# A second SwiGLU that starts with Strassen products, and casts in another order

## The chip, the cores and the metric

The kernel runs on one core of one Trainium2 chip. The metric is the device time of one execution in microseconds (us). The engines are TensorE (PE, matmuls), VectorE (DVE), ScalarE (ACT), GpSimd (POOL) and SyncE (SP, which issues most DMAs).

## The reference, cut to what matters

Two layers over 512 tokens with 1024 features, all in float32. Each layer is

```python
h = h + 0.5 * swiglu(rmsnorm(h, ffn1_norm[i]), ffn1_w_gu[i], ffn1_w_down[i])      # ffn1, hidden width 2816
u = rmsnorm(h, mix_norm[i])
...                                      # u @ w_in: conv branch, q/kv latents, two gates
merged = sigmoid(g_conv) * y_conv + sigmoid(g_mla) * y_mla    # y_mla: attention, 8 heads, block causal
h = h + merged @ w_o[i]
h = h + 0.5 * swiglu(rmsnorm(h, ffn2_norm[i]), ffn2_w_gu[i], ffn2_w_down[i])      # ffn2, the same shapes
h = h + sigmoid(rmsnorm(h, ple_norm[i]) @ w_ple_gate[i]) * (p[i] @ w_ple_proj[i])
```

where `swiglu(x) = (silu(x @ w_gate) * (x @ w_up)) @ w_down`. A final RMSNorm follows.

## The kernel before, in words

**Layout.** Everything is transposed: `h` is eight tiles `h[0..7]`, 128 features by 512 tokens each. To keep float32 accuracy on PE every operand is split into a high part (a cast to fp32r, on ACT) and a low part (the difference, on DVE), and one product is three matmuls: high x high, high x low, low x high (`mm3`, lines 212 to 214). Activations go through `split`/`split_to`, weights through `Stream.split` (lines 70 and 71), which handles 1024 columns (eight weight tiles of 128 x 128, a "half") at a time.

**Weights.** `Stream` reads halves from HBM in the order in which the program asks for them, into 10 raw buffers (`st`, and `s` for sums of weights); the cast parts `wh` and `wl` have 4 buffers each (`N_WH`). `W.get` hands out one 128 x 128 tile after another of the current half, so a projection can begin in the middle of a half.

**ffn.** For each hidden tile f of 22 the gate and up columns are multiplied with the normed h. The factor of the norm, `r`, comes from a sum of squares over all features (`Squares`, `rms`, matmuls with ones at lines 291 and 292) and is applied to the results, so the matmuls can begin before it is known. Two f make a pair n. A pair can be done whole (`projs`: 4 column tiles x 8 feature tiles x 3 matmuls of 512 tokens) or with seven Strassen-Winograd products (`Sevens`): tokens are cut in two halves of 256, features in two halves of 4 tiles, columns in two. A product is 4 feature tiles x 2 x 3 = 24 matmuls of 256 tokens. The token operands are built by `Halved.row(j)` out of h[j] and h[j+4]: products 1, 2, 3 take pieces of the normed h, 5 and 7 take halves of `t`, 6 and 4 halves of `u`. Product 1 uses the left half of h[j], product 5 the left half of `t`, which is the right half of h[j] minus its left; the other five need h[j+4]. The weight operands are built by `Quad.part` out of four quarters a11 to a22 on DVE: products 5, 6, 3 and 7 need a sum of weights first, and all seven a split. `step(n, j)` does product j of pair n and drains its PSUM bank; `finish` multiplies with r, applies silu and splits the result.

Before the change ffn2 does the first pair (f = 0, 1) whole (`n_whole = 2`) and pairs 1 to 10 as Strassen products. `early_rows` is off for ffn2: all four rows of `Halved` are built after the whole pair's first projections were issued. From pair 2 on, pieces of the down projection (`down`) stand between the products.

**Mixer.** Gates are Strassen products over four pairs; `conv_out(m)` (12 matmuls of 512 columns, then one DVE product) is placed between them, four for each of the last two pairs. `qkv(pr)` projects two heads: `q_rope` (and its rotation on ACT and DVE, `rope`), `key`, `query`, `values`, and casts each result; `scores` makes four score tiles of 128 queries for one head, 20 matmuls in all, and the softmax; `turn` transposes them, `mix_v` multiplies with the values. At the end W_o is applied for m = 0 to 7 and added into `h[m]`, and the next ffn's `normed` splits and squares each `h[m]` as it comes.

**Order.** PSUM has 8 banks, all from one pool, and the activations 60 tiles from one pool (`G`). A scheduler orders each engine's queue at build time: among the instructions whose operands and buffers are ready by its own estimates it takes the one that comes first in the program. On the chip every queue then runs in that order, and an instruction that waits holds all behind it.

Of the kernel before, what the change touches and what calls it, by code (L numbers as in the profile page):

```python
# [172 lines left out]
def trunk_kernel(ctx, tc, dims, x, p, positions, gains, rope_c, weights, out):  # L173
# [28 lines left out]
    def split_to(hi, lo, src, scale=None):  # L202
        if scale is None:
            nc.scalar.copy(hi, src)
            nc.vector.tensor_tensor(lo, src, hi.bitcast(F32), ALU.subtract)
        else:
            nc.scalar.activation(hi, src, AF.Copy, scale=scale)
            nc.vector.scalar_tensor_tensor(lo, src, scale, hi.bitcast(F32), ALU.mult, ALU.subtract)
# [35 lines left out]
    nc.gpsimd.dma_start(out=cols, in_=gains)  # L244
# [128 lines left out]
    class Halved:  # L373


        def __init__(self, nm, l, name):
            self.nm, self.l, self.name = nm, l, name
            self.ys = {p_: [] for p_ in range(1, 8)}

        def row(self, j, xs):  # L380
            H = S // 2
            left, right = slice(0, H), slice(H, S)
            name, k = self.name, j + KD // 2

            def halves_of(hi_lo, *ps_):
                for at, p_ in zip((left, right), ps_):
                    if p_:
                        self.ys[p_].append(tuple(t[:, at] for t in hi_lo))
# [6 lines left out]
            nc.vector.tensor_tensor(t13[:, left], xj[:, right], xj[:, left], ALU.subtract)  # L395
            nc.vector.tensor_tensor(t13[:, right], xk[:, right], xj[:, right], ALU.subtract)
            nc.vector.tensor_tensor(t24[:, left], t13[:, right], xj[:, left], ALU.add)
            nc.vector.tensor_tensor(t24[:, right], xk[:, left], t24[:, left], ALU.subtract)
            halves_of(split(t13, f"{name}t{j}"), 5, 7)
            halves_of(split(t24, f"{name}u{j}"), 6, 4)  # L400

    class Sevens:
# [17 lines left out]

        def product(self, ps, d, j):
            hi, lo = d["w"].part(j)
# [31 lines left out]
    def ffn(l, nm, name, first=False, beside=None, early=False):  # L454
# [20 lines left out]
        for f in range(n, n_whole):  # L475
            pss += projs(cs[f], xs, names[f])
        for j in range(n_early, KD // 2):
            ys.row(j, xs)

        def activate(f):  # L480
            g, u = G(f"{name}gn{f}"), G(f"{name}un{f}")
            nc.vector.tensor_tensor(g, pss[2 * f], r, ALU.mult)
            nc.scalar.activation(g, g, AF.Silu)
            nc.vector.tensor_tensor(u, pss[2 * f + 1], r, ALU.mult)
            nc.vector.tensor_tensor(u, u, g, ALU.mult)
            acts[f] = split(u, f"{name}a{f}")
# [18 lines left out]

# [504 lines left out]
```

## Time and profile before

| | |
|---|---|
| median of 3 runs | 2289.8 us (2289.72 to 2291.17) |
| the profiled execution | 2290.97 us, of which the span from first to last instruction is 2289.1 us |
| busy: PE, DVE, ACT, POOL | 2276.7, 1796.1, 1161.2, 34.7 us |
| matmuls | 14168 |
| read from HBM | 218.4 MB |

Times in rows are us from the start of the span. A row of the timeline gives start, duration, engine, source line, operation, output and inputs, shape, and in brackets how long the engine had been idle before it and what ended that. Matmuls overlap: the distance between two starts is what one costs, not its duration. The names b0, b1 are ffn2 of layer 0 and 1, a0, a1 ffn1, m0, m1 the mixer; `b01b` is bank b of pair 1 in b0, `m0s10p` the scores of head 0 of head pair 1 in m0.

### The profile page before, as it was taken

How to read it: one execution, taken by the hardware profiler on the slowest of the kernel's cores; microseconds unless marked ns; L12 is line 12 of the kernel's file. 1: busy time of each engine (PE TensorE's matmuls, PEld its weight loads, DVE VectorE, ACT ScalarE, POOL GpSimd, SP SyncE). 2: the span in 40 equal slices, each digit the busy share in tenths (PEclk: the TensorE clock that was granted, in tenths of full speed). 3: DMA queues.
4: the chain of work that ended last, by engine and by line, in shares of the span. 5: the costliest groups of instructions: out<-in, count | busy, mean ns of one | idle time of the engine just before them, and what ended most of it. 6: DMA issues, size and time to landing. Idle time of an engine off the chain costs nothing.

```text
span 2289.1 us, 34697 instructions
## 1 busy us (share of the span) xinstructions
PE 2276.7 (99%) x14168; PEld 2060.7 (90%) x14168; DVE 1796.1 (78%) x2508; ACT 1161.2 (51%) x1744; POOL 34.7 (2%) x43
## 2 busy tenths in 40 slices
PE   9999999999999999999999999999999999999998
PEld 8999988899888999998899999888988889999988
DVE  8887778877876988877798887768878669877765
ACT  7444445455743644444664444445467356444455
POOL 0000000000200000000000000000001000000000
PEclk9999999999999999999999999999999999999999
DMA  5333343134122233233223333322331123333321
GB/s 194 111 111 93 105 130 102 56 110 138 38 65 85 73 111 111 93 119 122 91 83 94 110 98 115 120 90 67 119 104 56 65 74 102 104 100 99 113 83 38
DMA packets 62975, 222.76 MB, mean 97 GB/s; under 512 B 7120, under 2 KB 7120, under 8 KB 62816
## 3 DMA queue, kind: packets, MB, share of 16 engines
q1 hardware_dynamic: 62208, 219.70, 30.4%
q8 instruction: 111, 1.82, 0.3%
q10 hardware_dynamic: 576, 0.79, 0.1%
q14 instruction: 48, 0.39, 0.1%
q0 software_dynamic: 32, 0.05, 0.0%
HBM read 218.42 MB, written 2.10 MB: 96 GB/s over the span
## 4 chain that ended last, share of the span: by engine, by line
PE 97%; DVE 2%; ACT 0%; issue 0%; DMA 0%; ACTq 0%; POOLq 0%
PE a0pd L212 2%; PE b0pd L212 2%; PE a1pd L212 2%; PE b1pd L212 2%; PE b1pd L213 2%; PE a1pd L213 2%; PE b0pd L213 2%; PE a0pd L213 2%; PE b1pd L214 2%; PE a1pd L214 2%; PE a0pd L214 2%; PE b0pd L214 2%; PE e1gp L212 1%; PE e1gp L214 1%; PE e1gp L213 1%; PE m0mop L212 1%
## 5 line engine op out<-in xcount | busy, mean ns | idle before, releaser
L70 ACT CAST wh<-st 128x1024 fp32r<-128x1024 f32 (+1 forms) x455 | 474.7, 1044 | 574.8 <-issue 57.7
L71 DVE TENSOR_TENSOR wl<-st,wh 128x1024 fp32r<-128x1024 f32 (+1 forms) x456 | 552.4, 1212 | 160.3 <-ACT wh L70 159.5
L70 ACT CAST wh<-s 128x1024 fp32r<-128x1024 f32 x94 | 98.8, 1051 | 132.6 <-PE b1pd L213 8.5
L71 DVE TENSOR_TENSOR wl<-s,wh 128x1024 fp32r<-128x1024 f32 x94 | 114.5, 1218 | 15.6 <-ACT wh L70 15.6
L149 DVE TENSOR_TENSOR st<-st,s 128x1024 f32<-128x1024 f32 x47 | 57.5, 1223 | 1.1
L146 DVE TENSOR_TENSOR s<-s,st 128x1024 f32<-128x1024 f32 x47 | 57.3, 1220 | 0.2
L141 DVE TENSOR_TENSOR s<-st,st 128x1024 f32<-128x1024 f32 x47 | 57.3, 1218 | 0.1
L152 DVE TENSOR_TENSOR st<-st,st 128x1024 f32<-128x1024 f32 x47 | 57.2, 1218 | 0.0
L511 DVE SCALAR_TENSOR_TENSOR h<-b0pd,h 128x512 f32<-128x512 f32 x40 | 27.5, 689 | 9.4 <-PE b0pd L214 9.2
L511 DVE SCALAR_TENSOR_TENSOR h<-b1pd,h 128x512 f32<-128x512 f32 x40 | 27.5, 688 | 9.4 <-PE b1pd L214 9.2
L511 DVE SCALAR_TENSOR_TENSOR h<-a1pd,h 128x512 f32<-128x512 f32 x40 | 27.5, 688 | 7.7 <-PE a1pd L214 7.7
L511 DVE SCALAR_TENSOR_TENSOR h<-a0pd,h 128x512 f32<-128x512 f32 x40 | 27.5, 687 | 6.4 <-PE a0pd L214 6.4
L106 POOL MEMSET wh<- 128x256 f32 x4 | 1.1, 313 | 1191.5 <-DVE wl L71 1191.5
L799 DVE TENSOR_TENSOR m1g<-m1mop,m1g 128x512 f32<-128x512 f32 x8 | 5.5, 690 | 6.5 <-PE m1mop L214 6.5
L799 DVE TENSOR_TENSOR m0g<-m0mop,m0g 128x512 f32<-128x512 f32 x8 | 5.5, 690 | 6.5 <-PE m0mop L214 6.5
L295 ACT ACT_TABLE_LOAD x8 | 10.3, 1283 | 0.1
L910 ACT ACTIVATE fsq<-h 128x256 f32<-128x256 f32 (+1 forms) x10 | 4.8, 480 | 9.9 <-DVE h L891 9.9
L804 DVE TENSOR_TENSOR h<-m0wop,h 128x512 f32<-128x512 f32 x8 | 5.5, 691 | 4.1 <-PE m0wop L214 4.1
L804 DVE TENSOR_TENSOR h<-m1wop,h 128x512 f32<-128x512 f32 x8 | 5.5, 690 | 4.1 <-PE m1wop L214 4.1
L621 DVE TENSOR_TENSOR m0z<-m0Vp,m0c 128x512 f32<-128x512 f32 x4 | 2.8, 692 | 6.2 <-PE m0Vp L214 6.2
L621 DVE TENSOR_TENSOR m1z<-m1Vp,m1c 128x512 f32<-128x512 f32 x4 | 2.8, 691 | 6.2 <-PE m1Vp L214 6.2
L650 DVE TENSOR_TENSOR m0g<-m0cop,m0g 128x512 f32<-128x512 f32 x8 | 5.5, 688 | 2.5 <-PE m0cop L214 2.5
(11171 smaller groups left out, 8787.5 us busy)
## 6 DMA issues: line engine op xcount, KB each, us to landing
st<-in_weights SPq DMA_DIRECT2D x406, 512.0 KB, 3.5
h<-in_x SPq DMA_DIRECT2D x8, 256.0 KB, 5.4
st<-in_weights SPq DMA_DIRECT2D x7, 256.0 KB, 5.3
out<-fo SPq DMA_DIRECT2D x7, 256.0 KB, 2.5
e0pi<-in_p SPq DMA_DIRECT2D x2, 256.0 KB, 3.7
e1pi<-in_p SPq DMA_DIRECT2D x2, 256.0 KB, 4.0
st<-in_weights ACTq DMA_DIRECT2D x1, 256.0 KB, 3.7
pos_i<-in_positions ACTq DMA_DIRECT2D x1, 256.0 KB, 3.8
```

What stands on the lines that cost most here:

```text
L70: self.nc.scalar.copy(hi[:, w], src[:, w])
L71: self.nc.vector.tensor_tensor(lo[:, w], src[:, w], hi[:, w].bitcast(F32), ALU.subtract)
L141: tt(self.s, self.a21, self.a22, ALU.add)
L146: tt(self.s, self.s, self.a11, ALU.subtract)
L149: tt(self.a12, self.a12, self.s, ALU.subtract)
L152: tt(self.a11, self.a11, self.a21, ALU.subtract)
L212: nc.tensor.matmul(ps, wh, vh, start=first, stop=False)
L213: nc.tensor.matmul(ps, wh, vl, start=False, stop=False)
L214: nc.tensor.matmul(ps, wl, vh, start=False, stop=last)
L511: nc.vector.scalar_tensor_tensor(h[m], ps, 0.5, h[m], ALU.mult, ALU.add)
L799: nc.vector.tensor_tensor(t, mla_ps[m], t, ALU.mult)
L804: nc.vector.tensor_tensor(h[m], ps, h[m], ALU.add)
```

## The change

1. **ffn2 in Strassen products from the first pair on** (`early=3`, `n_whole = 0`). `Halved.row` is cut in two: `own(j)` needs h[j] alone, `other(j)` needs h[j+4] too. During W_o `early_rows` calls `own` for rows 0 to 3 as h[0..3] come, and `other` for rows 0 to 2 as h[4..6] come; after h[6] the weight operands of products 1 and 5 of pairs 0 and 1 are split ahead (`sevens.split`). After h[7] comes `other(3)`. PE then does (0,1), (0,5), the sum of squares, (1,1), (1,5), and only then (0,2), (0,6), (0,3), (0,7), (0,4), (1,2), (1,6), (1,3) and the rest as before.
2. **Order by hand.** `tc.issue_after(ins)` puts what its block traces on the engine of `ins` behind `ins` in that engine's queue. The ACT drains of the first four products stand behind the multiplication for row 3; the DVE work of the other products up to (1,3), with the weight sums and splits, stands behind the last split of row 3 (`sums`).
3. **Mixer.** `conv_out(7)` moves from between the gate products to behind `qkv(0)`, ahead of the first scores. Since it hands out four weight tiles, `qkv(0)` now begins in the middle of a half, and its `values` come after the second query. In every `qkv` the two rotated query parts and the splits of the values are traced after all other parts.
4. **Launch.** The table of gains `cols` is loaded by SP, as its first DMA, where POOL did it.
5. ffn1 and the mixer build their rows through `own` and `other`, one behind the other: the same operations, `y` multiplied after the first difference.

The core of the diff:

```diff
-    nc.gpsimd.dma_start(out=cols, in_=gains)
+    nc.sync.dma_start(out=cols, in_=gains)
...
         def row(self, j, xs):
+            self.own(j, xs)
+            self.other(j, xs)
+        def own(self, j, xs, parts=False):
...
-            xj, xk, t13, t24 = (G(f"{name}{w}{j}") for w in "xytu")
-            nc.scalar.mul(xj, h[j], gain(self.nm, self.l, j))
-            nc.scalar.mul(xk, h[k], gain(self.nm, self.l, k))
-            halves_of(xs[j], 1, None)
-            halves_of(xs[k], 2, 3)
...
+            x, t = G(f"{self.name}x{j}"), G(f"{self.name}t{j}")
+            nc.scalar.mul(x, h[j], gain(self.nm, self.l, j))
+            nc.vector.tensor_tensor(t[:, left], x[:, right], x[:, left], ALU.subtract)
+            th, tl = G(f"{self.name}t{j}h", F32R), G(f"{self.name}t{j}l", F32R)
+            if parts:
+                split_to(th[:, left], tl[:, left], t[:, left])
+            self.ys[1].append(tuple(v[:, left] for v in xs[j]))
+            self.ys[5].append((th[:, left], tl[:, left]))
+            self.half[j] = x, t, th, tl, parts
+        def other(self, j, xs):
+            H = S // 2
+            left, right = slice(0, H), slice(H, S)
+            k = j + KD // 2
+            x, t, th, tl, parts = self.half.pop(j)
+            y, u = G(f"{self.name}y{j}"), G(f"{self.name}u{j}")
+            x_ins = nc.scalar.mul(y, h[k], gain(self.nm, self.l, k))
+            nc.vector.tensor_tensor(t[:, right], y[:, right], x[:, right], ALU.subtract)
+            nc.vector.tensor_tensor(u[:, left], t[:, right], x[:, left], ALU.add)
+            nc.vector.tensor_tensor(u[:, right], y[:, left], u[:, left], ALU.subtract)
+            at = right if parts else slice(0, S)
+            split_to(th[:, at], tl[:, at], t[:, at])
+            uh, ul = G(f"{self.name}u{j}h", F32R), G(f"{self.name}u{j}l", F32R)
+            last = split_to(uh, ul, u)
+            for p_, v, at in ((2, xs[k], left), (3, xs[k], right), (7, (th, tl), right), (6, (uh, ul), left), (4, (uh, ul), right)):
+                self.ys[p_].append(tuple(w[:, at] for w in v))
+            return x_ins.ins, last.ins
...
+        def split(self, n, j):
+            if n not in self.todo:
+                self.todo[n] = self.quad(n)
+            self.todo[n]["part", j] = self.todo[n]["w"].part(j)
         def product(self, ps, d, j):
-            hi, lo = d["w"].part(j)
+            hi, lo = d.pop(("part", j), None) or d["w"].part(j)
...
-    def ffn(l, nm, name, first=False, beside=None, early=False):
+    def ffn(l, nm, name, first=False, beside=None, early=2):
...
-        n_early = KD // 2 - 2 if early else 0
-        def early_rows(k, xs):
-            if KD // 2 < k + 1 <= KD // 2 + n_early:
-                ys.row(k - KD // 2, xs)
...
-        xs, acc = normed(nm, l, name, early_rows)
...
-        n_whole = 4 if first else 2
-        cs = [[W.col(nm + "_w_gu", l, c + f * P, D) for c in (0, DFF)] for f in range(n_whole)]
-        names = [[f"{name}p{w}{f}" for w in "gu"] for f in range(n_whole)]
-        n = 2 if first else 1
-        pss = projs(sum(cs[:n], []), xs, sum(names[:n], []), first)
-        r = rms(acc, D, name)
...
+        n_whole = 4 if first else 0 if early > 2 else 2
+        n0 = n_whole // 2
...
+        def early_rows(k, xs):
+            j = k - KD // 2
+            if n_whole == 0:
+                if j < 0:
+                    ys.own(k, xs, True)
+                elif j < early:
+                    ys.other(j, xs)
+                if k == KD - 2:
+                    for n in range(2):
+                        for j in (1, 5):
+                            sevens.split(n, j)
+            elif 0 <= j < early:
+                ys.row(j, xs)
+        xs, acc = normed(nm, l, name, early_rows)
+        if n_whole == 0:
+            x_ins, sums = ys.other(KD // 2 - 1, xs)
+            with tc.issue_after(x_ins):
+                step(0, 1)
+                step(0, 5)
+            r = rms(acc, D, name)
+            with tc.issue_after(x_ins):
+                step(1, 1)
+                step(1, 5)
+            order = (2, 6, 3)
...
+            for f in range(n, n_whole):
+                pss += projs(cs[f], xs, names[f])
+            for j in range(early, KD // 2):
+                ys.row(j, xs)
+            order = (1, 2, 5, 6, 3)
...
         np_ = nf // 2
-        n0 = n_whole // 2
         for f in range(n_whole - 2):
             activate(f)
-        step(n0, 1)
-        activate(n_whole - 2)
-        step(n0, 2)
-        step(n0, 5)
-        activate(n_whole - 1)
-        step(n0, 6)
-        step(n0, 3)
+        with tc.issue_after(sums) if n_whole == 0 else nullcontext():
+            for j in order:
+                if n_whole and j in (2, 6):
+                    activate(n_whole - (2 if j == 2 else 1))
+                step(n0, j)
...
             between = [(lambda m=m, f0=f0: down(m, f0, f0 + 4)) for m in range(4 * (n % 2), 4 * (n % 2) + 4)] if n > 1 else []
             for i, (n_, j_) in enumerate(((n + 1, 1), (n, 7), (n + 1, 5), (n, 4), (n + 1, 2), (n + 1, 6), (n + 1, 3))):
-                step(n_, j_)
+                if n == n_whole == 0:
+                    if j_ not in (1, 5):
+                        with tc.issue_after(sums):
+                            step(n_, j_)
+                else:
+                    step(n_, j_)
                 if i in (1, 2, 3, 5) and between:
                     between.pop(0)()
...
-            between = [(lambda m=m: conv_out(m)) for m in range(4 * n - 4, 4 * n)] if n else []
+            between = [(lambda m=m: conv_out(m)) for m in range(4 * n - 4, min(4 * n, KD - 1))] if n else []
             order = [(n + 1, 1), (n, 7), (n + 1, 5), (n, 4)]
             order += [(n + 1, j) for j in ((6, 2, 7, 3, 4) if n + 1 == n_last else (2, 6, 3))]
...
-                    vs.append(split(ps, f"{n}v{tb}"))
+                    vs.append(ps)
                 res["v"] = vs
...
-            def q_rope_parts():
+            def q_rope_parts(t):
                 qr = res["qr"]
...
-            query0 = lambda: query(0)
-            parts = [(3, q_rope), (2, lambda: key(0)), (3, query0), (2, lambda: key(1)), (3, lambda: query(1))]
+            parts = [(3, q_rope), (2, lambda: key(0)), (3, lambda: query(0)), (2, lambda: key(1)), (3, lambda: query(1))]
             at = [i for i in range(1, len(parts) + 1) if W.pairs_fit(2, sum(w for w, _ in parts[:i]))]
             parts.insert(at[-1], (4, values))
             for _, part in parts:
                 part()
-                if part is query0:
-                    q_rope_parts()
+            for t in range(2):
+                q_rope_parts(t)
+            res["v"] = [split(ps, f"{n}v{2 * i}") for i, ps in enumerate(res["v"])]
             return res
...
         qk = qkv(0)
+        conv_out(KD - 1)
         es = [scores(0, t, qk) for t in range(2)]
...
-        ffn(l, "ffn1", f"a{l}", l == 0, rotary if l == 0 else None, l > 0)
+        ffn(l, "ffn1", f"a{l}", l == 0, rotary if l == 0 else None, 2 if l else 0)
         mixer(l)
-        ffn(l, "ffn2", f"b{l}")
```

## Rows read from the trace of the kernel before

**Rows 1.** The page: busy time of the engines, and the granted clock of PE in 40 slices of the span (tenths of full speed, 9 is 90% or more).

```profile
PE 2276.7 (99%) x14168; PEld 2060.7 (90%) x14168; DVE 1796.1 (78%) x2508; ACT 1161.2 (51%) x1744; POOL 34.7 (2%) x43
...
PEclk9999999999999999999999999999999999999999
```

**Rows 2.** The waits of PE over the whole span: who waited for whom, us in total, times, longest.

```profile
PE a0pg L230 <- ACT a0x0h L207: 1.6, 1, 1.6
...
PE m0s10p L734 <- DVE m0h1qn1l L205: 0.9, 1, 0.9
PE m1s10p L734 <- DVE m1h1qn1l L205: 0.9, 1, 0.9
```

**Rows 3.** Timeline of PE from the end of W_o in layer 0: the first whole matmul of ffn2, the sum of squares, the second half of the whole pair, the first two Strassen products of pair 1.

```profile
742.53 0.39 PE L212 MATMUL b0pg<-b0x0h,wh 128*128 128x512 f32 x1
...
753.41 0.40 PE L291 MATMUL b0ps<-b0ah,ones 128*128 128x512 f32 x1
...
753.88 0.39 PE L212 MATMUL b0pg<-b0x0h,wh 128*128 128x512 f32 x1
...
764.78 0.28 PE L427 MATMUL b01b<-b0x0h,wh 128*128 128x256 f32 x1
...
767.66 0.28 PE L427 MATMUL b01a<-b0x4h,wh 128*128 128x256 f32 x1
```

**Rows 4.** DVE's busy time under W_o of layer 0, and from its end to the first product of pair 3 (window, its length, busy us and instructions, granted clock, DMA share, GB/s).

```profile
699.00:742.53 43.53, 26.73 (x32) 1.00 0.26 85
742.53:799.30 56.77, 53.61 (x77) 1.00 0.25 73
```

**Rows 5.** Timeline of DVE in a stretch without idle time: operations of 1024, 256 and 512 columns, one behind the other.

```profile
767.57 1.22 DVE L152 TENSOR_TENSOR st<-st,st 128x1024 f32<-128x1024 f32 x1
768.70 0.42 DVE L398 TENSOR_TENSOR b0u<-b0y,b0u 128x256 f32<-128x256 f32 x1
769.04 0.68 DVE L205 TENSOR_TENSOR b0t3l<-b0t,b0t3h 128x512 fp32r<-128x512 f32 x1
769.64 1.22 DVE L71 TENSOR_TENSOR wl<-st,wh 128x1024 fp32r<-128x1024 f32 x1
```

**Rows 6.** Timelines of ACT and DVE at the end of W_o in layer 0: a weight cast and the cast of the accumulated squares on ACT; h[7] and the last addition of squares on DVE.

```profile
742.55 1.06 ACT L70 CAST wh<-st 128x1024 fp32r<-128x1024 f32 x1 [1.67 <-PE m0wop L213]
...
746.16 0.62 ACT L204 CAST b0ah<-b0acc 128x512 fp32r<-128x512 f32 x1 [1.41 <-DVE b0acc L282]
...
742.73 0.69 DVE L804 TENSOR_TENSOR h<-m0wop,h 128x512 f32<-128x512 f32 x1 [0.59 <-PE m0wop L214]
...
745.44 0.68 DVE L282 TENSOR_TENSOR b0acc<-b0acc,b0sq 128x512 f32<-128x512 f32 x1
```

**Rows 7.** Timeline of PE in attention, layer 0 and then layer 1: the first score matmul of the layer and the first matmul behind its two sets; the third set (heads of pair 1, `s10`) from its first matmul over its wait to the first matmul behind it; the fifth set (`s20`) likewise.

```profile
566.61 0.28 PE L734 MATMUL m0s00p<-m0h0kn0h,m0h0qn0h 128*128 128x256 f32 x1
...
574.76 0.40 PE L212 MATMUL m0h1qr<-m0qn0h,wh 128*128 128x512 f32 x1
...
587.72 0.39 PE L734 MATMUL m0s10p<-m0h1kn0h,m0h1qn0h 128*128 128x256 f32 x1
...
589.45 0.39 PE L734 MATMUL m0s10p<-m0h1kn0h,m0h1qn0h 128*128 128x256 f32 x1 [0.87 <-DVE m0h1qn1l L205]
...
592.26 0.40 PE L764 MATMUL m0o00av<-m0pth,m0h0v0h 128*128 128x512 f32 x1
...
613.57 0.36 PE L734 MATMUL m0s20p<-m0h2kn0h,m0h2qn0h 128*128 128x256 f32 x1
...
616.88 0.40 PE L764 MATMUL m0o10av<-m0pth,m0h1v0h 128*128 128x512 f32 x1
...
1698.58 0.28 PE L734 MATMUL m1s00p<-m1h0kn0h,m1h0qn0h 128*128 128x256 f32 x1
...
1706.75 0.39 PE L212 MATMUL m1h1qr<-m1qn0h,wh 128*128 128x512 f32 x1
```

**Rows 8.** Timelines of PE, ACT and DVE ahead of the scores in layer 0: the first matmul of the projection of q; the last sigmoid of the gates and the four copies of the rotation on ACT; the split of the second kv tile, of the second query, and of the second query of head pair 1 on DVE.

```profile
554.79 0.40 PE L212 MATMUL m0h0qr<-m0qn0h,wh 128*128 128x512 f32 x1
...
559.77 0.73 ACT L646 ACTIVATE m0g<-m0g3t 128x256 f32<-128x256 f32 x2 [2.58 <-DVE m0g3t L641]
560.52 2.35 ACT L554 COPY m0h0qrt<-m0h0qr 32x512 f32<-32x512 f32 x4
...
557.84 0.69 DVE L205 TENSOR_TENSOR m0kvn1l<-m0kvt,m0kvn1h 128x512 fp32r<-128x512 f32 x1
...
571.53 0.68 DVE L205 TENSOR_TENSOR m0h0qn1l<-m0h0qn,m0h0qn1h 128x512 fp32r<-128x512 f32 x1
...
588.71 0.68 DVE L205 TENSOR_TENSOR m0h1qn1l<-m0h1qn,m0h1qn1h 128x512 fp32r<-128x512 f32 x1
```

**Rows 9.** Timeline of the launch: the first DMA issue of SP (h[0]), the issue of the gains on POOL, the first activation on ACT, the first real matmul; and, for the issues of h up to 14 us, the time from issue to landing.

```profile
0.73 0.38 SPq L53 DMA_DIRECT2D h<-in_x  x1
...
1.24 0.71 POOL L244 DMA_DIRECT2D cols<-in_gains  x1 [0.81 <-POOLq L999]
...
5.62 0.72 ACT L207 ACTIVATE a0x0h<-h,cols 128x512 fp32r<-128x512 f32 x1 [2.96 <-DMA cols<-in_gains]
...
6.40 0.80 PE L230 MATMUL a0pg<-a0x0h,wh 128*128 128x512 f32 x1 [1.57 <-ACT a0x0h L207]
...
DMA to landing us min/median/max: 3.5/5.4/5.5
```

More of the change, by code (lines that the diff above doesn't have):

```diff
@@ L1 @@
 import math
-from contextlib import ExitStack
+from contextlib import ExitStack, nullcontext
 import concourse.bass as bass
@@ L204, in split_to @@
             nc.scalar.copy(hi, src)
-            nc.vector.tensor_tensor(lo, src, hi.bitcast(F32), ALU.subtract)
+            return nc.vector.tensor_tensor(lo, src, hi.bitcast(F32), ALU.subtract)
         else:
             nc.scalar.activation(hi, src, AF.Copy, scale=scale)
-            nc.vector.scalar_tensor_tensor(lo, src, scale, hi.bitcast(F32), ALU.mult, ALU.subtract)
+            return nc.vector.scalar_tensor_tensor(lo, src, scale, hi.bitcast(F32), ALU.mult, ALU.subtract)
     def mm3(ps, w, v, first, last):
@@ L378, in __init__ @@
             self.ys = {p_: [] for p_ in range(1, 8)}
+            self.half = {}
         def row(self, j, xs):
+            self.own(j, xs)
+            self.other(j, xs)
+        def own(self, j, xs, parts=False):
             H = S // 2
             left, right = slice(0, H), slice(H, S)
[L383 to L388, printed above, removed]
@@ L398, in row @@
-            nc.vector.tensor_tensor(t24[:, right], xk[:, left], t24[:, left], ALU.subtract)
-            halves_of(split(t13, f"{name}t{j}"), 5, 7)
-            halves_of(split(t24, f"{name}u{j}"), 6, 4)
+            x, t = G(f"{self.name}x{j}"), G(f"{self.name}t{j}")
+            nc.scalar.mul(x, h[j], gain(self.nm, self.l, j))
+            nc.vector.tensor_tensor(t[:, left], x[:, right], x[:, left], ALU.subtract)
+            th, tl = G(f"{self.name}t{j}h", F32R), G(f"{self.name}t{j}l", F32R)
@@ L459, in ffn @@
         ys = Halved(nm, l, name)
-        n_early = KD // 2 - 2 if early else 0
-        def early_rows(k, xs):
-            if KD // 2 < k + 1 <= KD // 2 + n_early:
-                ys.row(k - KD // 2, xs)
-        xs, acc = normed(nm, l, name, early_rows)
-        n_whole = 4 if first else 2
-        cs = [[W.col(nm + "_w_gu", l, c + f * P, D) for c in (0, DFF)] for f in range(n_whole)]
-        names = [[f"{name}p{w}{f}" for w in "gu"] for f in range(n_whole)]
-        n = 2 if first else 1
-        pss = projs(sum(cs[:n], []), xs, sum(names[:n], []), first)
-        r = rms(acc, D, name)
[L475 to L486, printed above, removed]
+        n_whole = 4 if first else 0 if early > 2 else 2
+        n0 = n_whole // 2
         def finish(n, f, c, src, t):
@@ L504, in ffn, with activate @@
         step = sevens.step
+        def early_rows(k, xs):
[23 more added lines that the diff above has]
+        else:
+            cs = [[W.col(nm + "_w_gu", l, c + f * P, D) for c in (0, DFF)] for f in range(n_whole)]
+            names = [[f"{name}p{w}{f}" for w in "gu"] for f in range(n_whole)]
+            n = 2 if first else 1
+            pss = projs(sum(cs[:n], []), xs, sum(names[:n], []), first)
+            r = rms(acc, D, name)
+            for f in range(n, n_whole):
[3 more added lines that the diff above has]
+            order = (1, 2, 5, 6, 3)
+        def activate(f):
+            g, u = G(f"{name}gn{f}"), G(f"{name}un{f}")
+            nc.vector.tensor_tensor(g, pss[2 * f], r, ALU.mult)
+            nc.scalar.activation(g, g, AF.Silu)
+            nc.vector.tensor_tensor(u, pss[2 * f + 1], r, ALU.mult)
+            nc.vector.tensor_tensor(u, u, g, ALU.mult)
+            acts[f] = split(u, f"{name}a{f}")
         def down(m, f0, f1, ps=None, last=True, first_=True):
@@ L694, in q_rope @@
                 res["qr"] = rope(ps, cosT, sinT, n + "qr")
-            def q_rope_parts():
+            def q_rope_parts(t):
                 qr = res["qr"]
-                for t in range(2):
-                    q2 = G(f"{n}qr{t}", F32R)
-                    own, oth = slice(t * 64, t * 64 + 64), slice(64 - t * 64, 128 - t * 64)
-                    nc.scalar.copy(q2[own, :], qr[own, :])
-                    nc.vector.tensor_tensor(q2[oth, :], qr[own, :], q2[own, :].bitcast(F32), ALU.subtract)
-                    res["qr", t] = q2
+                q2 = G(f"{n}qr{t}", F32R)
+                own, oth = slice(t * 64, t * 64 + 64), slice(64 - t * 64, 128 - t * 64)
+                nc.scalar.copy(q2[own, :], qr[own, :])
+                nc.vector.tensor_tensor(q2[oth, :], qr[own, :], q2[own, :].bitcast(F32), ALU.subtract)
+                res["qr", t] = q2
             def key(t):
@@ L958, in trunk_kernel @@
     for l in range(DEPTH):
-        ffn(l, "ffn1", f"a{l}", l == 0, rotary if l == 0 else None, l > 0)
+        ffn(l, "ffn1", f"a{l}", l == 0, rotary if l == 0 else None, 2 if l else 0)
         mixer(l)
-        ffn(l, "ffn2", f"b{l}")
+        ffn(l, "ffn2", f"b{l}", early=3)
         ple(l, l == DEPTH - 1)
```

4 lines of the change are left out of this document (1 added, 3 removed).

## The prediction

> **What bounds the kernel now.** I read the page first: TensorE (PE) is busy 99% of the span at a granted clock of full speed, VectorE (DVE) 78% [rows 1]. So a time only changes where PE has fewer columns to stream or fewer holes. A busy share can't show small holes (the ends of matmuls are modelled), so the second view is who PE waited for: three entries count, one at the start for the first activations and one in each layer's attention [rows 2]. Third, PE in order of time, where the distance from start to start is the price: from 753.88 to 764.78 stand 48 matmuls of 512 columns, 0.227 us each; from there 24 of 256 columns take 2.88 us to 767.66, 0.120 each [rows 3]. There is no hole between the end of W_o at 742.53 and the first Strassen products. Fourth, DVE's load in that stretch: 53.6 us of 56.8 [rows 4]. It is the engine that could become the bound when PE's work shrinks. Last, the two places where PE does have holes: the first score matmuls [rows 7, 8] and the launch [rows 9].
>
> **The change part by part.**
>
> *Strassen for the first pair of ffn2.* Before, the gate and up tiles of f = 0 and 1 are 96 whole matmuls of 512 columns: 742.53 to 764.78 less the two matmuls of the sum of squares (753.41 to 753.88) is 21.78 us [rows 3]. Afterwards they are seven products of 24 matmuls: 7 x 2.88 = 20.16. PE saves 1.62 us a layer, 3.2 us in both, if nothing stalls. The Trainium skill speaks against it: "TensorE: Matmul & The Clock Gate", section "Back-to-back issue gap", gives 81 ns a matmul at 128 columns and 131 ns at 512 for a stream of weight loads and matmuls; a straight line between them, an estimate, makes 98 ns at 256. By that a pair would go from 96 x 131 = 12.6 us to 168 x 98 = 16.5, a loss of 3.9 us a layer. The trace disagrees: 227 and 120 ns, so each matmul pays some 13 ns beside its columns, and the pair gains.
>
> *What has to cover it.* The four products (0,1), (0,5), (1,1), (1,5) need only rows 0 to 3 of h, ready long before W_o ends. With the sum of squares they keep PE busy for 4 x 2.88 + 0.47 = 12.0 us, up to 754.5 on the old time axis. By then h[7] must have gone through its row and the weights of (0,2) must be split. From the rows: h[7] is written at 743.4; the accumulated squares are cast on ScalarE (ACT) at 746.16 [rows 6]. If the multiplication y of row 3 stands behind that cast, it ends near 747.4. Then DVE has three operations of 256 columns at 0.34, a split of 256 and one of 512 at 0.60 [rows 5], with a cast of ACT before each split: the last, the instruction `sums`, ends near 749.9. Every later weight operation of pair 0 on DVE stands behind it; (0,2) takes 1.13, so 751.0. That leaves 3.5 us. The tile pool for cast weights holds four, all four taken ahead; (0,2) gets the one that (0,1) gives back at 745.4, which is early enough.
>
> *DVE's load.* A pure pair costs DVE seven splits and four sums of 1024 columns, 11 x 1.13 = 12.4, and nine operations of 512 and four of 256 for its results, 6.8: 19.2 us against PE's 20.16. Up to the first product of pair 3 (799.30 before) PE will need 0.47 + 19 x 2.88 = 55.2 us. DVE needs there: h[7] and row 3 4.4; the norm's factor 1.2; 25 weight operations 28.3; results of pairs 0 and 1 13.6, the beginnings of pair 2 3.1. Sum 50.6, 92%, where it was 94% before without a hole in PE. The row work of four rows, some 10 us there before, has moved under W_o: 4 x 0.68 for `own`, 3 x 1.96 for `other`, one more sum, 9.7 us on top of 26.7 of 43.5 [rows 4]. That is 84%, hidden by W_o's matmuls; without that cover it is the fourth rival below. I take no stall; the other bound is 1.6 us a layer, the whole gain.
>
> *Attention: last convolution tile moved, other order of casts.* A clean set of scores is 3.31 us (613.57 to 616.88). The first two sets of the layer take 8.15 us instead of 6.62, the third 4.54: holes of 1.53 and 1.23 us, 2.8 us a layer; layer 1 has 8.17 at the same place [rows 7]. The first hole is late casts: the four copies of the rotation begin on ACT at 560.52 only, behind a sigmoid that waited 2.58 us for DVE, and the last cast of a query leaves DVE at 572.2, 5.6 us after the first score matmul [rows 8]. `conv_out(7)`, 12 matmuls, 2.72 us of PE, now stands between the projections and the scores. Everything ahead of it comes that much sooner on PE, and the results that DVE drains there too, so ACT's copies should begin 3 to 4 us earlier; the keys and queries are split ahead of the rotated parts and of the values. From the copies' end near 559 DVE then has three operations of the rotation, four splits, the rotated parts (two, 1.4 us) and two weight splits, 8 us and some waiting on casts, up to the first scores at 566.6: the hole shrinks to a few tenths, gain 1.3. The price of it: the projection of q now wants its inputs 2.72 us sooner, at 552.1 instead of 554.79, while the last split kvn1l was at 557.84 [rows 8]; from the end of product (3,2), three products of 2.88 ahead of 552.1 and so at 543.4, DVE has four weight splits, five splits of q and kv and six drains up to there, 4 x 1.13 + 11 x 0.60 = 11.1 us, so 554.7, against a first use near 555: even, at worst a few tenths lost. The values now come last in the first projection too, which covers the queries.
>
> The second hole ends with the split qn1l at 588.71 [rows 7, 8]: at that point four banks of PSUM hold transposes, two the values, one the query, one the first scores, all eight, and the query's is the next to come free. With the query split ahead of the rotated parts (1.4 us on DVE) it frees a bank about that much sooner, but the values hold theirs longer. I take 0.8 of 1.23. Together 2.1 us a layer, 4.2. Bounds: 0 (the wait only changes its name) and 5.5 (both holes gone in both layers).
>
> *Launch.* The first activation on ACT waits for `cols` until 5.62; it is issued on POOL at 1.24 and takes 4.4 us. On SP it goes out first, near 0.73, and h[0] second, one issue (0.38 us) later; h lands 3.5 us after its issue at best [rows 9]. Then h[0] is the later of the two, at 4.6 at the soonest, and the first real matmul comes up to 1.0 us sooner. I take 0.6, bounds 0 (h[0] lands as late as `cols` did) and 1.0. The loads behind it shift by 0.38 us too; that is hidden, since k = 1 is needed twelve matmuls, 2.7 us, after k = 0.
>
> Reordered rows in ffn1 and the mixer: same instructions, under PE that has no hole there: nothing; if DVE ran behind, 0.34 us each.
>
> Sum: 3.2 + 4.2 + 0.6 = 8.0 us. The profiled execution took 2290.97 (span 2289.1 and 1.9 around it), so 2283.0 on its own terms; the median of the runs is 2289.8, 1.2 lower, so 2281.8 there.
>
> **The rivals.** One measurement here can tell 0.2%, 4.6 us, from no change: faster is below 2285.2, slower above 2294.4.
>
> 1. Forecast, 2281.8, from 2279.8 to 2284.5: chance 0.55.
>
> 2. The holes in the scores stay: the banks of PSUM or the rotation's chain (copies 2.35 us, three operations, two splits) still end last. Only 3.2 + 0.6 remain: 2286.0, or 2284.6 with a third of the forecast gain. For it: eight banks are all in use, and values keep theirs longer. Against: both holes end with the split of a query on DVE, which now goes ahead of 1.4 us of other work or more. 0.22.
>
> 3. DVE becomes the bound in pairs 0 to 2: 92% leaves 4.6 us over 19 products, and each sum must wait for a cast. If 1.6 to 3 us a layer are lost, the Strassen gain is gone or reversed: 2285 to 2288. For it: 94% already; against: at 94% PE had no hole. 0.13.
>
> 4. Slower: `sums` comes late. All weight work of pair 0 on DVE is queued behind row 3. Each us by which it ends after 753.4 stops PE for one us. If the 9.7 us of row work did not fit under W_o and were done after it, `sums` would end at 759.6 and PE stand 6.2 us a layer, 12.4 in both: 2294.2; slower is decided from 6.3 us a layer on, and with row 3 behind two more splits it is 2296 to 2300. Against it: 84%. 0.07.
>
> 5. The matmuls of 256 columns cost more than 0.120 us beside the early products: at 0.130 (21.78 / 168) the gain is gone, 2285.0. 24 in a row at 0.120 say no [rows 3]. What decides is the ratio of a matmul of 256 columns to one of 512: even at 96/168 = 0.57, 0.53 in the rows. The Trainium skill's figures in the section named above make it 0.75, well beyond even; the rows do not agree. 0.03.
>
> **How the numbers follow.** Predicted 2281.8. Range 2279.8 (3.2 + 5.5 + 1.0 = 9.7 us, and 0.3 for the spread of the runs) to 2287.5, which takes in rivals 2 and 5 and most of 3. Faster by over 0.2%: nearly all of the first, a third of 2, 3 and 5: 0.66. Within: 0.27. Slower: 0.07.
>
> **What would show it.** In the profile afterwards: products of pair 0 right after W_o, each 2.88 us, with no matmul b0pg; DVE's split of u in row 3 ended within 7.5 us of W_o; no wait of PE for a weight split up to pair 3; the first two score sets near 6.7 us, the third under 4; the first activation on ACT before 5.3. Wrong would be a wait of PE for a weight split or for the third product, a wait at the projection of q for its inputs, or a score set that still takes over 4.5 us.

## The result and the profile after

The changed kernel takes 2299.19 us (median of 5 runs, 2297.52 to 2300.34) against 2289.8 beside it: ratio 1.0037, interval 1.0026 to 1.0049. It is 0.4% slower; 2281.8 us and faster was forecast, and the range ended at 2287.5. The profiled execution took 2297.52 us, its span 2295.3; it is the fastest of the five, and what follows is read from it.

The stages tell where it went. Each length is the distance between two matmul starts on PE's timeline: the mixer from its first gate product to W_o, ffn2 from the first matmul behind W_o to the first of the next stage.

| us | mixer, layer 0 | mixer, layer 1 | ffn2, layer 0 | ffn2, layer 1 | first real matmul at |
|---|---|---|---|---|---|
| before | 247.08 | 247.06 | 344.43 | 344.45 | 6.40 |
| after | 248.62 | 250.10 | 346.28 | 346.31 | 5.59 |

ffn2 was to become 1.62 us a layer shorter and became 1.85 longer; the mixer was to become 2.1 shorter and became 1.5 and 3.0 longer. The first ffn1 is 1.2 us shorter from its first real matmul on (not the launch's doing, see below); all other stages are as long as before, to 0.1 us. The waits of PE in the changed kernel, which answer to [rows 2], name both places:

```profile
PE b01a L450 <- ACT wh L70: 1.2, 1, 1.2
...
PE b11a L450 <- ACT wh L70: 1.1, 1, 1.1
...
PE m0s10p L787 <- DVE m0h1qr L752: 1.0, 1, 1.0
PE m1s10p L787 <- DVE m1h1qr L752: 0.9, 1, 0.9
...
PE m0s10p L784 <- DVE m0h1v0l L205: 0.8, 1, 0.8
PE m1s10p L784 <- DVE m1h1v0l L205: 0.8, 1, 0.8
PE b00b L450 <- DVE wl L71: 0.4, 1, 0.4
```

**ffn2.** PE's timeline, which answers to [rows 3]: W_o ends at 742.05 and the products follow at once, with no whole pair. At 763.35 product (0,7) begins (`b00b<-b0t0h`). PE's queue has two matmuls of (1,2) behind the first two of (0,7); they wait for their weight cast, and (0,7) then for its own weight split:

```profile
742.05 0.28 PE L450 MATMUL b00b<-b0x0h,wh 128*128 128x256 f32 x1
...
763.47 0.28 PE L450 MATMUL b00b<-b0t0l,wh 128*128 128x256 f32 x1
764.91 0.39 PE L450 MATMUL b01a<-b0x4h,wh 128*128 128x256 f32 x1 [1.16 <-ACT wh L70]
...
765.79 0.39 PE L450 MATMUL b00b<-b0t0h,wl 128*128 128x256 f32 x1 [0.39 <-DVE wl L71]
```

DVE's windows, to be read beside [rows 4]: 9 us from the end of W_o, then the rest up to 799.30.

```profile
742.05:751.05 9.00, 6.31 (x12) 1.00 0.00 1
751.05:799.30 48.25, 47.75 (x59) 1.00 0.39 121
```

DVE stands idle for 2.7 of the first 9 us and is full (99%) afterwards, so in this order it does not make up what it misses early. Its timeline shows for whom it waited, and what stands ahead of the late split:

```profile
746.67 0.69 DVE L282 TENSOR_TENSOR b0acc<-b0acc,b0sq 128x512 f32<-128x512 f32 x1 [0.99 <-ACT b0sq L281]
748.04 0.69 DVE L205 TENSOR_TENSOR b0al<-b0acc,b0ah 128x512 fp32r<-128x512 f32 x1 [0.69 <-ACT b0ah L204]
...
750.97 0.43 DVE L205 TENSOR_TENSOR b0t3l<-b0t,b0t3h 128x256 fp32r<-128x256 f32 x1 [0.95 <-ACT b0t3h L204]
751.49 0.69 DVE L205 TENSOR_TENSOR b0u3l<-b0u,b0u3h 128x512 fp32r<-128x512 f32 x1
...
761.32 1.22 DVE L146 TENSOR_TENSOR s<-s,st 128x1024 f32<-128x1024 f32 x1
...
762.78 1.22 DVE L152 TENSOR_TENSOR st<-st,st 128x1024 f32<-128x1024 f32 x1
...
764.52 1.22 DVE L71 TENSOR_TENSOR wl<-st,wh 128x1024 fp32r<-128x1024 f32 x1
```

`sums` (the split of u in row 3, 751.49) ends 10.1 us after W_o, and two sums of weights for pair 1 (L146, L152) go ahead of the split for (0,7) at 764.52. ACT in the same time explains the idle DVE (row of 746.67 and of 750.97):

```profile
745.05 1.05 ACT L70 CAST wh<-st 128x1024 fp32r<-128x1024 f32 x1 [1.28 <-PE b00b L450]
746.00 0.63 ACT L281 ACTIVATE b0sq<-h 128x512 f32<-128x512 f32 x1
...
748.66 1.28 ACT L295 ACT_TABLE_LOAD   x1
749.95 0.69 ACT L295 ACTIVATE b0r<-b0ps,eps_t 128x512 f32<-128x512 f32 x1
750.54 0.40 ACT L204 CAST b0t3h<-b0t 128x256 fp32r<-128x256 f32 x1
```

The cast of the weights of (0,2) waits 1.28 us for the buffer that (0,1) gives back, takes 1.05, and the squares of h[7], ready, stand behind it. Then the table load and the root for the norm's factor, 1.9 us, go ahead of the casts of row 3.

**Attention.** To be read beside [rows 7]: the first two sets of scores, then the third (`s10`) and the fifth (`s20`).

```profile
564.60 0.28 PE L784 MATMUL m0s00p<-m0h0kn0h,m0h0qn0h 128*128 128x256 f32 x1
...
571.73 0.50 PE L212 MATMUL m0h1qr<-m0qn0h,wh 128*128 128x512 f32 x1 [0.25 <-ACT m0s00e L793]
...
584.59 0.36 PE L784 MATMUL m0s10p<-m0h1kn0h,m0h1qn0h 128*128 128x256 f32 x1
...
586.50 0.39 PE L787 MATMUL m0s10p<-m0krh,m0h1qr 128*128 128x256 f32 x1 [0.95 <-DVE m0h1qr L752]
...
588.02 0.41 PE L784 MATMUL m0s10p<-m0h1kn0h,m0h1qn0h 128*128 128x384 f32 x1 [0.79 <-DVE m0h1v0l L205]
...
590.13 0.40 PE L814 MATMUL m0o00av<-m0pth,m0h0v0h 128*128 128x512 f32 x1
...
611.45 0.36 PE L784 MATMUL m0s20p<-m0h2kn0h,m0h2qn0h 128*128 128x256 f32 x1
...
614.75 0.50 PE L784 MATMUL m0s20p<-m0h2kn0h,m0h2qn0h 128*128 128x512 f32 x1 [0.35 <-DVE m0h2v0l L205]
...
616.01 0.39 PE L814 MATMUL m0o10av<-m0pth,m0h1v0h 128*128 128x512 f32 x1
```

The first two take 7.13 us where they took 8.15; the third takes 5.54 where it took 4.54, and it has a new wait, for the parts of the rotated queries (`m0h1qr`), ahead of one for a bank that the first value split (`m0h1v0l`) gives back. The fifth, clean before at 3.31 us, takes 4.56, and its last tile waits for a value split too; with the sixth (3.66 where it was 3.30) the third pair of heads loses 1.6 us a layer, more than the third set. ACT shows why the parts are late in the third set:

```profile
583.42 1.05 ACT L70 CAST wh<-st 128x1024 fp32r<-128x1024 f32 x1 [1.74 <-PE m0h1v L739]
584.37 1.26 ACT L751 CAST m0h1qr<-m0h1qrt 64x512 fp32r<-64x512 f32 x2
585.65 0.59 ACT L204 CAST m0h1v0h<-m0h1v 128x512 fp32r<-128x512 f32 x1
```

Ahead of them stands a cast of weights, which waits 1.74 us until PE's last value matmul gives a weight buffer back. In the kernel before the parts were cast ahead of this cast, at 584.40, and it waited for nothing:

```profile
586.34 1.05 ACT L70 CAST wh<-st 128x1024 fp32r<-128x1024 f32 x1
```

### The profile page after: what moved, and what is told of

It reads as the page before. It is cut to its first block, busy times and chain, and to the rows that moved or that the text cites. A ratio compares the mean times of both kernels' runs of the same rounds, so it can differ in the third digit from the quotient of the medians.

```text
span 2295.3 us, 35035 instructions
## 1 busy us (share of the span) xinstructions
PE 2276.9 (99%) x14312; PEld 2064.9 (90%) x14312; DVE 1818.8 (79%) x2540; ACT 1170.2 (51%) x1768; POOL 33.1 (1%) x42
## 4 chain that ended last, share of the span: by engine, by line
PE 94%; DVE 4%; ACT 1%; issue 1%; DMA 0%; SPq 0%; ACTq 0%
PE a1pd L212 2%; PE b1pd L212 2%; PE a0pd L212 2%; PE b0pd L212 2%; PE a1pd L213 2%; PE b1pd L213 2%; PE b0pd L213 2%; PE a0pd L213 2%; PE a0pd L214 2%; PE b1pd L214 2%; PE b0pd L214 2%; PE a1pd L214 2%; DVE wl L71 1%; PE e1gp L212 1%; PE e1gp L214 1%; PE e1gp L213 1%
## 5 line engine op out<-in xcount | busy, mean ns | idle before, releaser
L71 DVE TENSOR_TENSOR wl<-s,wh 128x1024 fp32r<-128x1024 f32 x98 | 119.4, 1218 | 12.8 <-ACT wh L70 12.8
L146 DVE TENSOR_TENSOR s<-s,st 128x1024 f32<-128x1024 f32 x49 | 59.8, 1220 | 0.2
L152 DVE TENSOR_TENSOR st<-st,st 128x1024 f32<-128x1024 f32 x49 | 59.7, 1219 | 0.0
L116 DVE TENSOR_TENSOR kl<-st,kh 128x512 fp32r<-128x512 f32 x10 | 6.8, 683 | 0.5 <-ACT kh L115 0.5
L701 DVE TENSOR_TENSOR m1g<-m1cop,m1g 128x512 f32<-128x512 f32 x8 | 5.5, 688 | 2.0 <-PE m1cop L214 2.0
```

The costliest lines, as they stand in the source:

```text
L71: self.nc.vector.tensor_tensor(lo[:, w], src[:, w], hi[:, w].bitcast(F32), ALU.subtract)
L146: tt(self.s, self.s, self.a11, ALU.subtract)
L152: tt(self.a11, self.a11, self.a21, ALU.subtract)
L701: nc.vector.tensor_tensor(gates[m], ps, gates[m], ALU.mult)
```

## The experiments

Each ratio is to runs of the kernel before made beside it (medians 2291.2 to 2291.5 us). Stage lengths are those of the table above, each from one profiled execution. The code shows the core of each edit; what stands behind # is a remark, not code.

**The four parts alone.** p1_launch: line 244 on SP. p2_ffn2: the diff of `Halved`, `Sevens` and `ffn`. p3_casts: the diff of `qkv`. p4_cop:

```
+            between = [(lambda m=m: conv_out(m)) for m in range(4 * n - 4, min(4 * n, KD - 1))] if n else []
...
         qk = qkv(0)
+        conv_out(KD - 1)
```

> Only the table of gains is issued on SP instead of POOL, everything else as in the kernel before. The prediction gave this 0.6 us (bounds 0 and 1.0), so 2289.2 us. The trace of the changed kernel shows TensorE's work of the first stage ending 2.0 us earlier relative to its own matmuls, with the full granted clock about 5 us earlier: if that is this edit's doing, 2287.8 us. If that came from something else in the changed program, 2289.2 or more.

> Only the second SwiGLU of both layers is as in the changed kernel; launch and attention as before. Theory A (the order on VectorE: sums of tokens, then the sums of pair 1's weights ahead of the split that product (0,7) needs): each layer pays 3.45 us of new waits for 1.62 us of saved columns, +1.8 a layer, 2293.4 us. Theory B (the loss of the changed kernel lies in the attention alone, and the waits here only stand where other waits stood): the 3.2 us saved stay, 2286.6 us.

> Only the order of casts in the attention is as in the changed kernel (the parts of the rotated queries and the splits of the values behind all keys and queries, for all pairs of heads); the eighth convolution output stays in the gate stage. Theory A (the parts and the values' banks now come late in each later pair): the third set of scores and those of the third pair wait some 1.0 + 0.9 us a layer more, while the first two sets gain nothing without the output behind them: 2 to 5 us slower, 2292 to 2295 us. Theory B (the order of casts is harmless and the move of the output is the loss): within 1 us of 2289.8.

> Only the eighth convolution output moves from the gate stage to stand ahead of the first scores; casts in the order of before. Theory A (it covers the wait ahead of the first scores as the prediction had it, 1.53 us to about 0.2 in each layer): 2.6 us faster, 2287.2 us. Theory B (the wait is only moved to a later set of scores or to the gates): within 0.5 us of 2289.8. Theory C (the output's read by VectorE delays the casts of the first scores): 1 to 2 us slower.

| | median us | ratio | interval | mixer, both layers | ffn2, both layers |
|---|---|---|---|---|---|
| p1_launch | 2290.06 | 0.9994 | 0.9985 to 1.0004 | 247.10, 247.12 | 344.48, 344.46 |
| p2_ffn2 | 2296.04 | 1.0020 | 1.0011 to 1.0029 | 247.07, 247.10 | 346.31, 347.46 |
| p3_casts | 2296.30 | 1.0025 | 1.0016 to 1.0035 | 249.35, 249.45 | 344.45, 344.53 |
| p4_cop | 2287.59 | 0.9982 | 0.9973 to 0.9992 | 245.19, 245.18 | 344.47, 344.46 |

The moved output gains 1.9 us a layer by itself, ffn2 loses 1.9 (3.0 in the second layer, where the clock falls, see the last section), and the order of casts loses 2.3. In the last three the direction is theory A's; its times were counted from 2289.8 us, where the kernel before took 2291.2 beside these runs. Whether the order on VectorE is the cause in ffn2, as theory A of p2_ffn2 says, this run can't tell. In p4_cop the first two sets of scores take 6.47 us (565.27 to 571.74), with the old casts: the move alone closes the first hole. The launch alone can't be told from no change by its time; in its trace the first real matmul starts at 5.52 instead of 6.40. The other 1.2 us that the trace of the changed kernel shows there are the moment at which PE's matmuls of 512 columns go from 0.43 us apart to 0.23: 9.5 us in before and in p1_launch alike, 5.9 in the changed kernel's profiled execution. That is not this edit's doing: in p4_cop, with the launch of before, the moment is 6.7, and in p7_best (below), with the launch changed, 9.4.

**ffn2: order or lateness?** p5_order holds the weights of pair 1 behind the split for (0,4); p6_act works on ACT's queue alone:

```
p5:  if (n_, j_) == (0, 4):
+        sums = W.last
...
p6:  with tc.issue_after(cast):            # cast: ACT's cast of u in row 3
+        r = rms(acc, D, name)
...
+    with tc.issue_after(sums), tc.issue_after(x_ins):      # for (0,2), (0,6), (0,3)
```

> The second SwiGLU alone (launch and attention as before), with one change: the sums and splits of the weights of pair 1 stand on VectorE behind the split for product (0,4), and so no longer ahead of the split for (0,7). Theory A (the order of the queue costs the waits): in the run with the SwiGLU alone, 2296.0 us, the splits of (0,7) stood behind two sums of pair 1, 2.45 us, and TensorE waited 1.96 us there; they go, the 0.3 us holes stay: 2292 us. Theory B (VectorE is behind because row 3 ends late, and any order leaves the same lack): the wait moves to (0,4) or (1,2), at most 1 us is won, 2295 us or more.

> The second SwiGLU alone with another change: on ScalarE the weight cast for (0,2), which stood ahead of the squares of h[7] and held them back some 2.2 us, and the factor of the norm (with its table load of 1.28 us), which stood ahead of the casts of row 3, now stand behind them; VectorE's order is as in the changed kernel, with the sums of pair 1 ahead of the split for (0,7). Theory B (late row 3): its last split ends some 2 us sooner, everything behind it on VectorE too, and the wait of 1.96 us at (0,7) goes: 2292 us. Theory A: the sums of pair 1 still stand ahead, a wait over 1 us stays there: 2294 us or more.

p5_order: 2294.95 us, ratio 1.0016 (1.0007 to 1.0026), ffn2 346.45 and 346.47. The wait at (0,7) is gone and stands elsewhere, as theory B has it, though mostly at (1,3), which theory B did not name; PE's waits there:

```profile
PE b11c L450 <- DVE wl L71: 1.3, 1, 1.3
PE b01c L450 <- DVE wl L71: 1.3, 1, 1.3
```

p6_act: 2291.39 us, ratio 1.0000 (0.9990 to 1.0009), ffn2 344.53 and 344.52, 1.8 us a layer less than in the change. W_o ends at 743.76 in its trace, `sums` near 752.0, 8.3 us later, and DVE in the first 9 us:

```profile
743.76:752.76 9.00, 7.89 (x14) 1.00 0.00 1
752.76:801.01 48.25, 47.92 (x60) 1.00 0.40 122
```

1.6 us more of DVE's time is used, and about as much is won, as theory B has it. How much of it the weight cast gives and how much the norm's factor, no run tells. The pair still only breaks even.

**Both orders mended, on the parts that gain.** p7_best is p5_order and p6_act together with the launch and the moved output, casts as before.

> Both mended orders in the second SwiGLU together, with the moved convolution output and the gains on SP, and the casts of the attention in the order of before. If the parts add up: 2291.2 of the kernel before in these runs, less 3.2 (columns) plus 0.7 (small holes that stay), less 3.7 (output), less 0.9 (launch): 2284 us. If VectorE has no room for the all-Strassen SwiGLU in any order: 2286.5 us, no better than the moved output and the launch alone.

2283.43 us, ratio 0.9965 (0.9952 to 0.9978); ffn2 342.92 and 342.91. The 1.5 us a layer of the columns are there after all, and no wait of ffn2 is among PE's longest:

```profile
PE idle L320 <- DVE hpi L250: 1.0, 1, 1.0
PE m0s10p L789 <- DVE m0h1v0l L205: 1.0, 1, 1.0
PE m1s10p L789 <- DVE m1h1v0l L205: 1.0, 1, 1.0
PE fss L978 <- DVE fsq L959: 0.8, 1, 0.8
PE a0pg L230 <- ACT a0x0h L207: 0.6, 1, 0.6
```

DVE up to the first product of pair 3, the stretch for which the prediction summed up its load:

```profile
740.06:795.32 55.26, 53.92 (x71) 1.00 0.30 97
```

It is busy for 53.9 us of 55.3, and PE has no hole over 0.1 us there. So the order of pair 1's weights matters too, but only once row 3 is in time: alone it won nothing, on top of p6_act 1.6 us a layer.

**The casts: which half?** On top of p4_cop, p8_vals defers only the splits of the values, p9_parts only the parts:

```
p8:  res["v"] = [split(ps, f"{n}v{2 * i}") for i, ps in enumerate(res["v"])]     # at the end of qkv
p9:  for t in range(2):
         q_rope_parts(t)                                                        # at the end of qkv
```

> The moved convolution output, and of the new order of casts only the splits of the values, traced behind all keys and queries; the parts of the rotated queries stand where they were. Theory A (the parts, put behind keys, queries and a weight split, are what costs): within 1 us of the 2287.6 us with the output moved alone. Theory B (the values hold their two banks longer, and the scores of the next pair wait for a bank): 1 us a layer or more, 2289.6 us or above.

> The convolution output moved as in the changed kernel, and of the new order of casts only the other half: the parts of the rotated queries behind all keys and queries; the values are split where they were. Theory A (the parts alone cost it): in the changed kernel the parts of the second pair of heads come 1.1 us too late for its first scores, ahead of the 1 us wait for a bank that stands there anyway, and the third pair's some 1 us: 2287.6 us with the output moved, plus 2 to 3.4 a layer, 2291.6 to 2294.4 us. Theory B (neither half costs anything alone, only both together): within 1 us of 2287.6.

p8_vals: 2288.38 us, ratio 0.9989 (0.9979 to 0.9999), mixer 245.17 and 245.15. p9_parts: 2288.55, ratio 0.9989 (0.9979 to 0.9998), mixer 245.64 and 245.61. The theory that the parts cost it falls: alone they cost 0.45 us a layer, the values nothing. Together, on the moved output, they cost 3.4 (248.62 less 245.19). PE's timeline in p9_parts shows how it escapes: the parts come later still, but PE goes on with the other products of all four score tiles, and the parts' matmuls stand last.

```profile
587.85 0.50 PE L732 MATMUL m0s10p<-m0h1kn0h,m0h1qn0h 128*128 128x512 f32 x1 [0.31 <-DVE m0h1v2l L205]
...
588.65 0.30 PE L735 MATMUL m0s10p<-m0krh,m0h1qr 128*128 128x256 f32 x1
...
589.72 0.40 PE L736 MATMUL m0s10p<-m0krl,m0h1qr 128*128 128x512 f32 x1
```

That takes a bank for each score tile. In the change the values hold theirs until after the parts; PE begins two tiles, stands for the parts, and the third tile waits for the value split (rows of 586.50 and 588.02 above). That the banks are what joins the two halves is read from these rows; no run gives the kernel more banks.

**Everything but the casts, and everything with one cast moved.** p10_nocasts is the change with `qkv` of before. p12_cast is the whole change with the weight cast of 583.42 put behind the parts:

```
+            if pr == 1:
+                W.behind = 2, cast        # the third split from here issues behind ACT's last cast of the parts
```

> The whole change with the casts of the attention in the order of before. If the parts of the change add up: 2291.4 us of the kernel before, less 0.9 (launch), less 3.7 (output moved), plus 4.7 (SwiGLU as in the change): 2291.5 us, and all of the rest up to the 2299.2 of the change, 7.7 us, is the order of casts on top of the moved output. If part of the loss is a thing between launch, SwiGLU and output that no part shows alone: 2294 us or more.

> The whole change with one cast moved: the cast of weights for the fourth pair of heads on ScalarE, which stands ahead of the parts of the second pair's rotated queries and waits 1.74 us for the last value matmul to give its buffer back, and so VectorE's difference behind it, stands behind the parts and the values. Theory A (this one cast holds the parts, 1.11 us, and behind them the values' banks, 0.95 us, in the third set of scores of each layer): both waits go, about 2 us a layer, and with them the stretch of 1.5 us at half the clock that follows them in the second layer of the changed kernel's trace: 2294 to 2295 us against 2299.2. Theory B (the order of casts costs it in other places as well or the wait only comes from the next operation in the queue): 2297 us or more.

p10_nocasts: 2292.32 us, ratio 1.0005 (0.9996 to 1.0015), mixer 245.47 and 245.17: without the new casts 6.9 us of the loss are gone, although its ffn2 is 1.2 us a layer longer than the change's (last section). p12_cast: 2293.32, ratio 1.0009 (1.0000 to 1.0019), mixer 246.82 and 246.81: moving one cast takes 5.9 us off the median. In the traces it is 5.1 us, 1.8 in the first layer and 3.3 in the second, of which 1.5 are the clock (last section). ACT in p12_cast:

```profile
581.71 1.26 ACT L759 CAST m0h1qr<-m0h1qrt 64x512 fp32r<-64x512 f32 x2
583.00 0.59 ACT L212 CAST m0h1v0h<-m0h1v 128x512 fp32r<-128x512 f32 x1
...
585.93 1.05 ACT L76 CAST wh<-st 128x1024 fp32r<-128x1024 f32 x1
```

The parts are cast 2.66 us earlier, in the time in which ACT had waited for the buffer, and no `s10` is among PE's waits. The third set takes 3.72 us (584.70 to 588.42), 0.8 less than in p4_cop, so theory A holds there. Against p4_cop 1.6 us a layer remain all the same: some 0.8 in the first pair of heads and 1.6 in the third. They go with the new casts (p10_nocasts has a fifth set of 3.30 us), and neither half of these makes them alone (3.31 in p8_vals, 3.54 in p9_parts); which cast holds the third pair no run tells.

**The third set, on the best version.** p11_vhold is p7_best with DVE's split of weights that stood ahead of the second pair's values put behind them.

> The kernel with both mended orders in the SwiGLU, the moved output, the launch and the casts of before (2283.4 us), with one change: a split of weights for the fourth pair of heads, which VectorE did for 1.13 us just ahead of the splits of the second pair's values, stands behind them. Theory A (the third set of scores waits for a bank that the first value split gives back): the 1.1 us there go in each layer, 2281.3 us. Theory B (the bank, or ScalarE's cast of the same weights ahead of the value's, holds it anyway, or the split is late for its own use): within 0.7 us of 2283.4.

2282.50 us, ratio 0.9961 (0.9947 to 0.9975), mixer 244.72 and 244.43: 0.7 us a layer, less than theory A's 1.1, and no `s10` is left among PE's waits. The third set itself is 1.1 us shorter (3.45 where p7_best has 4.54), but the fourth is 0.25 longer. It has the lowest median of all; by time alone it can't be told from p7_best, and both are ahead of before and of the change.

## Why the prediction was wrong

Two steps failed. In ffn2 it was the cover of row 3: `sums` was to end 7.4 us after W_o, with no stall behind it; it ended 10.1 us after, and PE stood for 3.5 us a layer. In attention it was the order of casts, priced as part of the gain: on top of the moved output it costs 3.4 us a layer, 1.6 of them in the third pair of heads, which the sum had at nothing.

*Strassen for the first pair* was right: a product still takes 2.88 us (24 matmuls at 0.120), no `b0pg` is left, and with the waits gone (p7_best) ffn2 is 1.5 us a layer shorter where 1.62 was forecast. The sustained figures of the Trainium skill in "TensorE: Matmul & The Clock Gate", section "Back-to-back issue gap", by which, as an estimate, the pair would lose 3.9 us, don't hold here: the rows have 227 and 120 ns.

*What has to cover it* failed, and that decided ffn2. I set row 3's multiplication behind one cast on ACT. I had read from the change that weight work stands behind `sums`, but that holds on DVE's queue only: the weight casts on ACT were free to go ahead of the squares. The one for (0,2) gets its buffer 3.0 us after W_o, as forecast ("early enough"), but the queue stands while it waits (1.28 us) and is cast (1.05). I also left out the table load and the root, 1.9 us on the same queue. p6_act moves just these and wins 1.8 us.

*DVE's load* was summed too low: 50.6 us of 55.2 (92%), where p7_best has 53.9 of 55.3 (98%). Yet PE has no hole there, so the load by itself was not the stall. p6_act and p7_best use the same DVE time (7.89 and 7.90 us of the first 9, 47.9 and 48.0 of the next 48.25) and differ by 1.6 us of PE: at such a load the start and the order decide, and the sum had neither. Rival 3 (0.13) and rival 4 (0.07) name the place. Rival 4's rule does not fit, though: it counts from 753.4, and `sums` ended at 752.7 on its axis, which would cost nothing; of the 3.5 us, 2.1 fell at (0,7), 21 us behind W_o. Its own row (work under W_o that doesn't fit) was not the cause either.

*Attention* was wrong in size and in sign. The first hole: forecast 1.3 us a layer gained, from the move and the casts together; the move alone gains 1.9 (p4_cop), and the casts give some of it back (7.13 us for the two sets where p4_cop has 6.47). The second hole: 0.8 us gained was forecast, since the query's split goes ahead of the parts. It does, but the wait only changed its name, as rival 2 has it for no gain, and the set grew by 1.0. What I had not looked at was the wait for a weight buffer on ACT: put behind that cast, the parts wait with it. The third pair of heads had no hole before, and I gave it no term; the same order costs 1.6 us there. The price of the output's move at the projection of q, a few tenths at worst, was right: nothing was lost (its sum, 543.4 + 11.1, is 554.5 and not 554.7, which changes nothing).

*Launch*: the first activation starts at 4.81 and the first real matmul at 5.59, 0.8 us sooner where I took 0.6. The loads behind it were not hidden, though: at 8.44 PE loses 0.5 us at the second tile of h, which it does not in p4_cop, at the same pace and with the launch of before. The launch can't be told from no change by time (p1_launch), so this term is shown by traces alone.

## What to carry to other kernels

When work is held back by an order on one engine, follow the same work on the other engine that prepares it: its half of the job is not held, and takes a place in that queue, with its wait for a buffer. An engine can be busy for 98% of a stretch without holding another up, as DVE in p7_best, but only if its first operation is in time and its queue in the order of need. Casts that look out of the way may fill an idle time in which the queue would otherwise wait, and two delays that cost little alone may cost much together.

## What the chip did that I had not expected

After two holes of PE close together (0.95 and 0.79 us in attention, 1.2 and 0.4 at (0,7)) its granted clock sometimes falls for some 3 us. In the second layer of the changed kernel (windows of PE, clock behind the count of instructions):

```profile
1721.00:1723.00 2.00, 0.74 (x4) 1.00 0.17 57
1723.00:1725.00 2.00, 1.70 (x7) 0.80 0.50 205
1725.00:1727.00 2.00, 2.00 (x6) 0.50 0.00 0
1727.00:1729.00 2.00, 2.00 (x13) 0.84 0.00 0
```

0.50 is the 1.2 GHz level; ahead of it PE had stood twice in the third set of scores. The matmuls of 512 columns start 0.43 us apart there instead of 0.23, and the stage is 1.5 us longer than in layer 0, where the same two holes stand and no stretch is at the lower level. The mixer's 3.0 us in layer 1 are so 1.5 of waits and 1.5 of clock. p2_ffn2 (second layer) and p10_nocasts (both) have the same behind the waits at (0,7), with windows at 0.53 and 0.50, and their ffn2 is 1.2 us longer than in the change; p3_casts has the holes in attention in both layers and, in its profiled execution, no such stretch. A hole can cost more than its length, but not each time; what decides it stays open.
